# Weight sums pinned in program order, and merge-stage pools that wait tile by tile, in a hybrid encoder block

## The chip, the cores and the metric

The kernel runs on one core of a Trainium2 chip. The time is device microseconds from launch to end; three runs of the kernel before were made, and one more execution was profiled. The engines are TensorE (PE, with its weight loads as PEld), VectorE (DVE), ScalarE (ACT), GpSimd (POOL) and SyncE (SP), which issues all the DMAs here. Each engine takes its instructions in the order in which its queue holds them.

## The reference, cut to what matters

One block of a bidirectional encoder on 1040 tokens (16 meta tokens and 1024 real ones) of width 1024: a normalised input is projected, goes through four heads of chunked retention and through a chunked state-space mixer (SSD) of 32 heads in 4 groups, and the two results are gated, merged, projected and added; then comes a gated feed-forward part with a convolution.

```python
def hybrid_layer(h, pos, norm_mix_w, w_in, ret_gn_w, w_ret_out, ...):
    u = rms_norm(h, norm_mix_w)
    q, k, v, g_ret, z, xbc, dt_f, dt_b, gate_ret, gate_ssd = _split(u @ w_in, IN_SIZES)
    ...
    y_ret = bidirectional_retention(pad_front(q), pad_front(k), pad_front(v), log_gamma)[:, PAD:]
    y_ret = head_group_norm(y_ret).reshape(b, l, RET_V) * ret_gn_w
    y_ret = (jax.nn.silu(g_ret) * y_ret) @ w_ret_out
    ...
    y_ssd = group_rms_norm(y, ssd_norm_w, SSD_GROUPS) @ w_ssd_out
    merged = jax.nn.sigmoid(gate_ret) * y_ret + jax.nn.sigmoid(gate_ssd) * y_ssd
    h = h + merged @ w_out
    f = dw_conv_centred(rms_norm(h, norm_ffn_w) @ w_ffn_up, w_ffn_conv, b_ffn_conv)
    fg, fu = _split(f, (D_FF, D_FF))
    return h + (jax.nn.silu(fg) * fu) @ w_ffn_down
```

## The kernel before

Every float32 product is done as three matmuls on operands split into a high and a low part (`mm3`, lines 143 to 145). A weight is loaded by SP into one of two `wraw` tiles (line 132), split by ACT into `whi` (line 135) and by DVE into `wlo` (line 136), three of each. `fm` makes 8 x 3 matmuls of up to 348 columns into one of three PSUM banks `psd`.

The kernel runs in stages. After the input norm come the four retention heads. The steps of a head's recurrence (`ret_steps`) are interleaved by `merge` with the dense projections of the next head (`ret_dense`; for the last head those of z), by costs that are written into the list. In a head POOL does the product of the rotary sum (`sw`, line 338), the two scalings of q per chunk (`qd`, line 429), and the addition and the power of the chunk's norm (`bs`, lines 448 and 449); DVE makes the normalised chunk `ry` from that (line 451), PE transposes it (`ptr`, line 459), DVE gates it and SP stores it (`yr`, line 467).

The feed-forward product uses sums of blocks of its up-projection weights. They are made in this stage, beside the heads, and kept in DRAM (`ws_d`) until then. `sum_steps` (from line 488) makes them in 44 units: `load` brings two tiles of 128 x 2 x 256 (256 KB each, lines 499 and 500), `add` does four POOL operations in place (lines 506 to 509), `store` writes both tiles back (line 513). The tiles have two buffers each. `spread` puts the steps of 12 units evenly among the dense steps of each of the heads 0 to 2 and the remaining 8 units among those of head 3, with a cost of 0.

The program text is not the order on the engines. A scheduler walks the program with a model of the chip's times and lets each engine issue, at each moment, the earliest traced instruction that is ready in the model; an instruction whose inputs the model takes as landed can go ahead of work that is traced before it. `tc.keep_in_program_order(ins)` ties an instruction behind the one that was traced just before it on its engine, for the order of issue alone.

After the heads comes SSD, group by group, whose last steps for a chunk write `yt` tiles (ACT, line 912) and store them to `ys_d` (line 914). Gate projections (`gate_steps`, lines 291 and 292) run beside it; six steps of them (`last_gates`) are kept for the change to the merge stage. There `kblock` loads the retention result in halves into three `ka` buffers (line 983), ACT casts them to `krh` (line 984) and DVE makes `krl` (line 985), eight tiles each; then `gated` does the product with `w_ro` and scales it by the gate (line 995), and the two SSD products follow, then `w_o` with the residual rows `xr`.

SBUF room is taken in pools that open and close. With the default, the first use of a new pool waits until every earlier pool that held any of its bytes is done with; with `reuse_waits="tile"` each tile waits for the earlier tiles on its own bytes alone. By the sizes in order of allocation, `sg` (the `ka` and `gt` tiles) lies on the bytes of `tok`; `hb` on the end of `tok`, `dec` and the first SSD tiles; `krh` on `bt`, `ct`, `x0`, `x1`, `x2` and `yb`; `krl` on `br`, then the small tiles and `t1` (tile 3 and 4), the two `yt` buffers (tiles 4 and 5), and room of the convolution that is long done. The pools of the feed-forward part (`ob`, `wx`, `fp`) have `reuse_waits="tile"` already.

Of the kernel before, what the change touches and what calls it, by code (L numbers as in the profile page):

```python
# [12 lines left out]
ALU = mybir.AluOpType  # L13
# [82 lines left out]
def hybrid_kernel(ctx, tc, t):  # L96
    nc = tc.nc
# [84 lines left out]
    ws_d = [dr.tile([P, 2, 1024], F32, name=f"ws_{j}", tag=f"ws_{j}") for j in range(NF)]  # L182
# [305 lines left out]
    def sum_steps(us):  # L488


        steps = []

        def part(src, s_):
            return src.rearrange("p (h s c) -> p s h c", h=2, s=2)[:, s_]

        def load(u):
            j, s_ = u // 2, u % 2
            a, b = [rb[0].tile([P, 2, 256], F32, name=f"ws{i}", tag=f"ws{i}", bufs=2) for i in range(2)]
            nc.sync.dma_start(out=a, in_=part(t["w_up"][j], s_))
            nc.sync.dma_start(out=b, in_=part(t["w_up"][NF + j], s_))  # L500
            wsum[u] = a, b

        def add(u):
            a, b = wsum[u]
            a11, a12, a21, a22 = a[:, 0, :], a[:, 1, :], b[:, 0, :], b[:, 1, :]
            nc.gpsimd.tensor_tensor(a22, a21, a22, op=ALU.add)
            nc.gpsimd.tensor_sub(a21, a11, a21)  # L507
            nc.gpsimd.tensor_sub(a11, a22, a11)
            nc.gpsimd.tensor_sub(a12, a12, a11)

        def store(u):
            for i, x in enumerate(wsum.pop(u)):
                nc.sync.dma_start(out=part(ws_d[u // 2][:, i, :], u % 2), in_=x)

        for u in us:
            if u == 0:
                steps += [(0.0, lambda: load(0)), (0.0, lambda: load(1))]
            steps += [(0.0, lambda u=u: add(u)), (0.0, lambda u=u: store(u))]
            if u + 2 < 2 * NF:
                steps.append((0.0, lambda u=u: load(u + 2)))  # L520
        return steps
# [441 lines left out]
    cv_es.close()  # L963
    ssd_es.close()
    tp.close()
    sg = ctx.enter_context(tc.tile_pool(name="sg", bufs=2))
    hp = ctx.enter_context(tc.tile_pool(name="hp", bufs=1))
    hb = hp.tile([P, KT, NB + 2], F32, name="hb")
    nc.gpsimd.memset(hb[:, :, NB:NB + 2], 0.0)
    h2 = [hb[:, d, :] for d in range(KT)]  # L970
    phL = ExitStack()
    lp = phL.enter_context(tc.tile_pool(name="lp", bufs=1))
    HN = NB // 2

    def kblock(pool, name, src):
# [23 lines left out]
    run(last_gates[1:])  # L999
    phA.close()  # L1000
    phR = ExitStack()
    bp = phR.enter_context(tc.tile_pool(name="bp", bufs=1, side="right"))
    for d in range(KT):
        w = wload(t["w_ro"][d])
        for b, (t0, n) in enumerate(BLK_B):
# [11 lines left out]
            sops1 = kblock(lp, "kr", lambda k: ys_d[2 + k // 4][:, k % 4, :])  # L1017
    phR.close()
    phM = ExitStack()
    mp = phM.enter_context(tc.tile_pool(name="mp", bufs=1, side="right"))  # L1020
    mh, ml = [], []
    for d in range(KT):
        w = wload(t["w_so"][2 * d + 1])
# [13 lines left out]


    oa_es = ExitStack()
    oa = oa_es.enter_context(tc.tile_pool(name="oa", bufs=1))  # L1040
    OPS = ("b11", "t2", "t1", "t3", "b21", "t4", "b22")

    def op_tiles(pool, r):
# [2 lines left out]

    ops = [op_tiles(oa, 0), None]
    wo_es = ExitStack()
    wo = wo_es.enter_context(tc.tile_pool(name="wo", bufs=2, side="right"))

    def row_rms(x, n):

# [413 lines left out]
def _build(tc, args):  # L1466
    with ExitStack() as ctx:
        hybrid_kernel(ctx, tc, args)
# [15 lines left out]
```

## Time and profile before

| | |
|---|---|
| median of three runs | 2555.64 us (2548.39 to 2556.68) |
| the profiled execution | 2567.85 us, span 2566.1 us |
| mean granted clock of PE | 0.964 |
| busy share of the span | PE 94%, PEld 88%, DVE 51%, ACT 33%, POOL 30% |
| mean DMA traffic | 126 GB/s |

All rows are times of the one profiled execution, in us from the start of its span. The heads run from about 50 to 535 us, SSD to about 1440, the merge stage to about 1800, the feed-forward part to the end. A wait is listed with the engine and line that waited, what it waited for, the sum in us, how often, and the longest.

### The profile page before, as it was taken

What the parts mean: (1) busy time and instruction counts of PE and PEld (TensorE: products, weight loads), DVE (VectorE), ACT (ScalarE), POOL (GpSimd) and SP (SyncE); (2) the same over time, 40 slices, a digit from 0 to 9 for tenths busy, and PEclk for the clock granted to TensorE, in tenths of its full rate; (3) what the DMA queues carried; (4) which work ended last, traced back from release to release, by engine and by line L of the source; (5) the groups of instructions that cost most, each with busy time, mean ns of one, the idle gap of its engine ahead of it and who ended that gap; (6) DMA issues with size and microseconds to landing.
All of it is one profiled execution on the core that took longest, in us unless ns stands there. A gap on an engine that the chain in (4) does not pass through costs nothing.

```text
span 2566.1 us, 39997 instructions
## 1 busy us (share of the span) xinstructions
PE 2405.6 (94%) x15888; PEld 2248.8 (88%) x15888; DVE 1306.4 (51%) x1917; ACT 850.2 (33%) x1462; POOL 782.4 (30%) x933
## 2 busy tenths in 40 slices
PE   7776899999989989999998899999999999999997
PEld 7766799998779878887988799999899999998887
DVE  6122243364563564365346344343797777774435
ACT  4211221133344253244323422122554444442114
POOL 3566622212561462364145112222111111110002
PEclk9988999999989999998999899999999999999998
DMA  4666621212482375157246655335444444454211
GB/s 160 201 217 200 206 68 46 60 54 78 142 176 63 125 163 103 65 168 155 50 134 170 167 166 150 90 95 167 148 144 128 116 119 116 120 170 175 72 44 66
DMA packets 197227, 324.46 MB, mean 126 GB/s; under 512 B 22128, under 2 KB 125040, under 8 KB 192944
## 3 DMA queue, kind: packets, MB, share of 16 engines
q1 hardware_dynamic: 197040, 321.91, 43.4%
q8 instruction: 125, 2.05, 0.3%
q14 instruction: 62, 0.51, 0.1%
HBM read 241.57 MB, written 80.27 MB: 125 GB/s over the span
## 4 chain that ended last, share of the span: by engine, by line
PE 69%; DMA 11%; POOL 8%; DVE 6%; ACT 3%; issue 3%; SPq 1%; POOLq 0%; DVEq 0%; ACTq 0%
PE psu L1194 17%; PE psd L143 12%; PE psd L145 12%; PE psd L144 11%; DMA ws<-in_w_up 4%; PE psw L144 3%; PE psw L145 3%; PE psw L143 3%; DMA br<-row 2%; PE pss L807 1%; POOL ws L507 1%; PE psb L828 1%; PE psy L442 1%; DMA ws<-ws 1%; POOL t L878 1%
## 5 line engine op out<-in xcount | busy, mean ns | idle before, releaser
L143 PE MATMUL psd<-uh,whi 128*128 128x342 f32 (+3 forms) x1376 | 469.9, 342 | 9.6 <-ACT gs L291 5.0
L144 PE MATMUL psd<-ul,whi 128*128 128x342 f32 (+3 forms) x1376 | 448.7, 326 | 0.0
L145 PE MATMUL psd<-uh,wlo 128*128 128x342 f32 (+3 forms) x1376 | 447.7, 325 | 0.0
L135 ACT CAST whi<-wraw 128x1024 fp32r<-128x1024 f32 (+1 forms) x144 | 149.2, 1038 | 510.3 <-PE psd L144 300.9
L136 DVE TENSOR_TENSOR wlo<-wraw,whi 128x1024 fp32r<-128x1024 f32 (+1 forms) x144 | 190.3, 1323 | 206.3 <-ACT whi L135 206.1
L143 PEld LDWEIGHTS psd<-uh,whi 128*128 128x128 f32 (+1 forms) x1376 | 266.4, 194 | 20.4 <-issue 7.9
L144 PEld LDWEIGHTS psd<-ul,whi 128*128 128x128 f32 (+1 forms) x1376 | 265.6, 193 | 7.7 <-issue 7.4
L145 PEld LDWEIGHTS psd<-uh,wlo 128*128 128x128 f32 (+1 forms) x1376 | 264.8, 192 | 0.1
L143 PE MATMUL psd<-whi,uh 128*128 128x256 f32 x768 | 235.7, 307 | 0.4 <-ACT uh L219 0.4
L145 PE MATMUL psd<-whi,ul 128*128 128x256 f32 x768 | 218.5, 285 | 3.2 <-POOL ul L221 2.7
L144 PE MATMUL psd<-wlo,uh 128*128 128x256 f32 x768 | 219.0, 285 | 0.0
L143 PEld LDWEIGHTS psd<-whi,uh 128*128 128x128 f32 x768 | 148.7, 194 | 11.3 <-issue 8.8
L144 PEld LDWEIGHTS psd<-wlo,uh 128*128 128x128 f32 x768 | 148.9, 194 | 6.1 <-issue 5.5
L145 PEld LDWEIGHTS psd<-whi,ul 128*128 128x128 f32 x768 | 148.1, 193 | 3.9 <-POOL ul L221 3.1
L144 PE MATMUL psw<-ahl,whi 128*128 128x512 f32 (+1 forms) x400 | 149.5, 374 | 1.6 <-DVE ahl L1313 1.6
L143 PE MATMUL psw<-ahl,whi 128*128 128x512 f32 (+1 forms) x400 | 147.5, 371 | 0.0
L145 PE MATMUL psw<-ahl,wlo 128*128 128x512 f32 (+1 forms) x400 | 146.6, 368 | 0.0
L143 PE MATMUL psd<-krh,whi 128*128 128x342 f32 x384 | 124.2, 324 | 3.3 <-ACT krh L984 3.3
L144 PE MATMUL psd<-krl,whi 128*128 128x342 f32 x384 | 124.2, 324 | 0.1
L145 PE MATMUL psd<-krh,wlo 128*128 128x342 f32 x384 | 124.0, 323 | 0.0
L1253 DVE SCALAR_TENSOR_TENSOR hb<-hb,vec 128x1024 f32<-128x1024 f32 x88 | 111.2, 1281 | 0.4 <-ACT hb L1249 0.2
L854 DVE TENSOR_TENSOR br<-br,tok 128x2048 f32<-128x2048 f32 (+1 forms) x36 | 83.5, 2319 | 48.9 <-DMA br<-row 48.9
(306 smaller groups left out, 6151.7 us busy)
## 6 DMA issues: line engine op xcount, KB each, us to landing
br<-row SPq DMA_DIRECT2D x32, 1024.0 KB
ws<-in_w_up SPq DMA_DIRECT2D x88, 256.0 KB
ws<-ws SPq DMA_DIRECT2D x88, 256.0 KB
gt<-gate SPq DMA_DIRECT2D x72, 171.0 KB
wraw<-in_w_xbc SPq DMA_DIRECT2D x24, 512.0 KB
wraw<-ws SPq DMA_DIRECT2D x47, 256.0 KB
hb<-ws SPq DMA_DIRECT2D x45, 256.0 KB
act<-hb SPq DMA_DIRECT2D x22, 512.0 KB
```

What stands on the lines that cost most here:

```text
L135: nc.scalar.copy(hi[:, :n], raw[:, :n])
L136: nc.vector.tensor_sub(lo[:, :n], raw[:, :n], hi[:, :n].bitcast(F32))
L143: nc.tensor.matmul(ps, ah, bh, start=(i == 0), stop=False)
L144: nc.tensor.matmul(ps, ah, bl, start=False, stop=False)
L145: nc.tensor.matmul(ps, al, bh, start=False, stop=(i == n - 1))
L442: nc.tensor.matmul(py[:n, :256], a, b, start=(i == 0), stop=(i == len(mms) - 1))
L507: nc.gpsimd.tensor_sub(a21, a11, a21)
L807: nc.tensor.matmul(ps, bk(c), st[("xw", d, c)][:n], start=True, stop=True)
L828: nc.tensor.matmul(ps[:n, :], tk("ct", c - 1), st[("pb", c)], start=True, stop=True)
L854: nc.vector.tensor_tensor(r, r, tok[:n, c, 0, g * 16:g * 16 + 16].unsqueeze(2).broadcast_to([n, 16, n]), op=ALU.add)
L1194: nc.tensor.matmul(ps[:, :n], a[:, c], b[:, k, :], start=start and k + i == 0, stop=k == 3 and i == 2, skip_group_check=True)
L1253: nc.vector.scalar_tensor_tensor(o[half], f[half][:, 1 + tap:1 + tap + SEQ], V("fconv_w", 3 * fi + tap), o[half], op0=ALU.mult, op1=ALU.add)
```

## The change

Each unit's first POOL addition and both its stores are pinned behind the instruction traced before them on POOL and on SP. The loads and the other three POOL operations are as before. Seven pools that open at or after the change from SSD to the merge stage (`sg`, `hp`, `lp`, `bp`, `mp`, `oa`, `wo`) get `reuse_waits="tile"`. No operation is added or removed.

```diff
         def add(u):
             a, b = wsum[u]
             a11, a12, a21, a22 = a[:, 0, :], a[:, 1, :], b[:, 0, :], b[:, 1, :]
-            nc.gpsimd.tensor_tensor(a22, a21, a22, op=ALU.add)
+            tc.keep_in_program_order(nc.gpsimd.tensor_tensor(a22, a21, a22, op=ALU.add))
             nc.gpsimd.tensor_sub(a21, a11, a21)
             nc.gpsimd.tensor_sub(a11, a22, a11)
             nc.gpsimd.tensor_sub(a12, a12, a11)
 
         def store(u):
             for i, x in enumerate(wsum.pop(u)):
-                nc.sync.dma_start(out=part(ws_d[u // 2][:, i, :], u % 2), in_=x)
+                tc.keep_in_program_order(nc.sync.dma_start(out=part(ws_d[u // 2][:, i, :], u % 2), in_=x))
...
-    sg = ctx.enter_context(tc.tile_pool(name="sg", bufs=2))
-    hp = ctx.enter_context(tc.tile_pool(name="hp", bufs=1))
+    sg = ctx.enter_context(tc.tile_pool(name="sg", bufs=2, reuse_waits="tile"))
+    hp = ctx.enter_context(tc.tile_pool(name="hp", bufs=1, reuse_waits="tile"))
...
-    lp = phL.enter_context(tc.tile_pool(name="lp", bufs=1))
+    lp = phL.enter_context(tc.tile_pool(name="lp", bufs=1, reuse_waits="tile"))
...
-    bp = phR.enter_context(tc.tile_pool(name="bp", bufs=1, side="right"))
+    bp = phR.enter_context(tc.tile_pool(name="bp", bufs=1, side="right", reuse_waits="tile"))
...
-    mp = phM.enter_context(tc.tile_pool(name="mp", bufs=1, side="right"))
+    mp = phM.enter_context(tc.tile_pool(name="mp", bufs=1, side="right", reuse_waits="tile"))
...
-    oa = oa_es.enter_context(tc.tile_pool(name="oa", bufs=1))
+    oa = oa_es.enter_context(tc.tile_pool(name="oa", bufs=1, reuse_waits="tile"))
...
-    wo = wo_es.enter_context(tc.tile_pool(name="wo", bufs=2, side="right"))
+    wo = wo_es.enter_context(tc.tile_pool(name="wo", bufs=2, side="right", reuse_waits="tile"))
```

## Rows read from the trace of the kernel before

**Rows 1.** The page's 40 slices of 64 us: PE busy and granted clock, in tenths.
```profile
PE   7776899999989989999998899999999999999997
PEclk9988999999989999998999899999999999999998
```
**Rows 2.** Windows: length, busy us (instructions) of PE, PEld, DVE, ACT, POOL; clock, DMA share, GB/s.
```profile
75.00:325.00 250.00, 188.50 (x1180) 175.99 (x1179) 64.18 (x147) 49.28 (x106) 159.24 (x230) 0.90 0.67 208
325.00:525.00 200.00, 199.68 (x1351) 189.10 (x1350) 77.67 (x203) 40.87 (x90) 44.93 (x92) 0.99 0.18 53
```
**Rows 3.** Tile ws: ns min/median/max, first and last start; then POOL's idle time before it.
```profile
L506 POOL TENSOR_TENSOR ws<-ws x44: 721/733/1713, 57.8 to 315.4; 128x256 f32<-128x256 f32 x44
...
  DMA ws<-in_w_up: 85.6, 46
```
**Rows 4.** Windows of the three longest stalls of PE in the heads.
```profile
117.50:135.00 17.50, 0.59 (x4) 0.19 (x2) 0.95 (x2) 2.05 (x5) 9.60 (x14) 0.65 0.64 189
182.50:190.00 7.50, 0.00 (x0) 0.00 (x0) 0.55 (x2) 0.00 (x0) 5.19 (x10) 0.84 0.71 236
242.50:260.00 17.50, 0.91 (x3) 0.51 (x4) 3.17 (x8) 0.55 (x2) 10.27 (x18) 0.59 0.65 172
```
**Rows 5.** Waits from 75 to 325 us, of DVE and PE: us in total, times, longest.
```profile
DVE ry L451 <- POOL bs L449: 90.7, 12, 11.6
DVE rk L339 <- POOL sw L338: 45.0, 7, 18.8
...
PE ptr L459 <- DVE ry L451: 36.3, 10, 13.1
```
**Rows 6.** Timeline of POOL: start, us, operation, [idle before it and what ended it].
```profile
123.78 0.72 POOL L506 TENSOR_TENSOR ws<-ws 128x256 f32<-128x256 f32 x1 [3.27 <-DMA ws<-in_w_up]
...
127.55 0.92 POOL L338 TENSOR_TENSOR sw<-sw,sin 128x348 f32<-128x348 f32 x1
```
**Rows 7.** Waits of SP's DMA queue over the whole span.
```profile
SPq L467 <- DVE ryt L465: 58.0, 13, 7.8
```
**Rows 8.** Pieces of the chain that ended last: start, us, what (a store, a load).
```profile
90.27 3.62 DMA ws<-ws
93.91 5.95 DMA ws<-in_w_up
```
**Rows 9.** Timelines of POOL and DVE around one long add.
```profile
173.95 1.63 POOL L507 TENSOR_TENSOR ws<-ws,ws 128x256 f32<-128x256 f32 x1 [1.13 <-DMA ws<-in_w_up]
...
173.77 2.90 DVE L136 TENSOR_TENSOR wlo<-wraw,whi 128x1024 fp32r<-128x1024 f32 x2
```
**Rows 10.** Windows at the change to the merge stage and after it.
```profile
1447.50:1455.00 7.50, 2.54 (x12) 2.26 (x11) 2.54 (x4) 2.95 (x5) 0.11 (x1) 0.70 0.21 35
1455.00:1465.00 10.00, 10.00 (x57) 9.73 (x57) 4.66 (x7) 4.92 (x9) 0.00 (x0) 0.88 0.86 250
1465.00:1472.50 7.50, 4.09 (x14) 3.01 (x13) 3.69 (x5) 3.78 (x8) 0.00 (x0) 0.67 0.83 239
1472.50:1480.00 7.50, 7.50 (x34) 7.50 (x33) 2.22 (x4) 2.82 (x5) 0.00 (x0) 0.65 0.69 217
1480.00:1800.00 320.00, 320.00 (x2159) 320.00 (x2158) 125.34 (x181) 70.16 (x98) 72.62 (x79) 1.00 0.45 134
```
**Rows 11.** Chain that ended last, at the change to the merge stage.
```profile
1438.75 12.53 DMA ys<-yt
1451.37 0.63 ACT krh L984
...
1452.81 3.40 DMA ka<-yr
...
1457.60 3.63 DMA ka<-yr
```
**Rows 12.** Timeline of SP's DMA queue: the first loads of the retention result.
```profile
1431.10 1.54 SPq L983 DMA_DIRECT2D ka<-yr  x3
```
**Rows 13.** Waits of PE from 1420 to 1480 us.
```profile
PE psd L143 <- ACT gs L291: 5.0, 1, 5.0
```

## The prediction

> **What bounds the kernel now.** I read the 40 slices of the page first: the reader is to see that TensorE (PE) is busy at nine tenths nearly everywhere, and that the exceptions are the first five slices (to 320 us), a few eights later, two of them side by side (1411 to 1540 us), and the last slice; the granted clock is below full in most of these [rows 1]. So the end is set by PE, and an edit is worth what PE idles, or does at its lower clock, in the stage it touches.
>
> The windows view puts numbers on the retention stage. From 75 to 325 us PE is busy 188.5 of 250 us at a granted clock of 0.90, and DMA stands at 0.67; from 325 to 525 us, with the same kind of work for heads 2 and 3, PE is busy 199.7 of 200 [rows 2]. What differs is where the 44 weight sums lie: the first add starts at 57.8 us and the last unit at 315.4 [rows 3], although the program text spreads them over all four heads. So before the change the sums ran ahead, 257.6 / 43 = 6.0 us a unit.
>
> Why does that stop PE? Three long stalls carry 41 of the 61.5 us [rows 4]. The waits of that stretch name VectorE (DVE) waiting for GpSimd (POOL): the normalised chunk waits 90.7 us for the power on POOL, the rotary sum 45.0 us for POOL's product, and PE's transpose waits for the chunk [rows 5]. POOL's own order shows the reason: the rotary product of 127.55 us stands behind adds that had to wait for their loads [rows 6], and POOL waits for those loads 46 times, 85.6 us [rows 3]. POOL takes its queue in order, so whatever stands behind such an add is late.
>
> **Part 1, the adds and stores pinned.** The first add of each unit goes behind the POOL instruction traced before it, which hangs on PE's progress through its head, and so does each store on SP. The other three adds depend on the first; the two loads are not pinned, but with two buffers the load of unit u+2 needs the stores of unit u landed. So loads, adds and stores of all units are spread. No work is removed: 176 adds, 88 loads, 88 stores remain. The bound of the gain is what PE loses now. Idle: 61.5 us. Clock: 250 x (1 - 0.90) = 25 us of deficit, of which the three stalls hold 17.5 x 0.35 + 7.5 x 0.16 + 17.5 x 0.41 = 14.5 us, where PE was idle anyway; about 10 us were matmuls at the lower level. Sum 71 us.
>
> What is late next? After the change the stage would last from 57.8 to 525 - 71 = 454, or 396 / 44 = 9.0 us a unit, against the 6.0 us at which the chain of units can run. The loop of a buffer pair is: four adds of 0.73 us, 2.9 [rows 3]; on SP the store stands behind a yr store, which now makes the queue wait 13 times, 58.0 / 13 = 4.5 us each, 7.8 at most [rows 7]; a store landing 3.6 and a load 6.0 [rows 8]. Without the yr wait that is 12.5 us, near the present 2 x 6.0; with it 17.0 us against two units, 18.0: it fits, narrowly; at 7.8 it is 20.3, and the add stands waiting 2.3 us. Queued behind that add on POOL are the power of the chunk, the rotary product and the two scalings of q; DVE waits for the first two, PE for DVE. How much wait does PE not see? Before, DVE waited 90.7 / 12 = 7.6 us each time and PE 36.3 / 10 = 3.6 [rows 5], so some 4 us are covered; and from 325 us on PE loses nothing although the same chain runs there [rows 2]. One unit of 2.9 us is covered. Unit plus 2.3 is 5.2, so 1.2 us too long. If every unit did that, 44 x 1.2 = 53 us would come back and 18 us of gain remain; if none did, 71. I take the 13 units whose queue now waits for a yr store: 13 x 1.2 = 16 us, a gain of 55 us.
>
> The DMAs move too: the traffic that made 0.67 goes into a stretch at 0.18 [rows 2], which only shortens landings. Weight loads that stand behind a pinned store wait one unit's adds, 2.9 us; their cover is the three split weights ahead of PE, each 72 matmuls (36 to 72 for the token-major ones), 5 to 11 us at 320 / 2159 = 0.148 us [rows 10], so nothing; without that cover it would be 2.9 us for each load that meets one. The last unit ends before the last yr stores in program order, and those are waited for already when the next stage opens; nothing there.
>
> A rule of the Trainium skill speaks against the spreading. The row first: an add that meets a two-input subtraction on DVE took 1.63 us instead of 0.73 [rows 9, 3]. The page "SBUF — State Buffer", section "SBUF: two separate sides", says that DVE and GpSimd share one port pair as an exclusive lock, which a DVE operation with two SBUF inputs takes against a GpSimd operation that reads SBUF. The trace agrees for those adds. By the rule alone, adds placed beside DVE's work would all be long; that is a rival below.
>
> **Part 2, pools that wait tile by tile.** Two PE gaps at the change of stage: 1447.5 to 1455 us (busy 2.5 of 7.5) and 1465 to 1472.5 (4.1 of 7.5), and matmuls at the lower clock behind each [rows 10]. The chain shows a ys store of 12.53 us, and then the first cast of krh [rows 11]. Its input had been issued at 1431.10 [rows 12]; it waited for the whole SSD pool, whose yt tiles that store reads. ScalarE stood with it, and behind it on ScalarE the gate that frees a PSUM bank: PE waited 5.0 us for that [rows 13]. By room, krh0 to krh3 and krl0 to krl3 lie on tiles done by about 1430; only krl4 and krl5 lie on yt. So casts can start at 1431.1 + 3.4 = 1434.5 [rows 11, 12]. Then the three buffers of ka turn over once in 1457.60 - 1452.81 = 4.8 us [rows 11]: sixteen halves are 5.3 turns, 26 us, done at 1460.5, or 1465 if the ys stores slow the loads by 4.5 us (my estimate, a turn). The gates without a stall end at 1465 - 5.0 (idle) - 1.2 (10 us at a clock of 0.88 [rows 10]) = 1459. By 1480 the retention product has done 14 + 34 matmuls, less some 4 of the last gate, at 0.148 us [rows 10], 6.5 us of work, so it began in effect at 1473.5; after, between 1461 and 1467 with 2 us for a clock fallen once. Gain 6 to 12, I take 9. Ends: 14 if the clock stays up and krh is ready at 1459; minus 5 if the casts, now early in ScalarE's queue, wait for ka with the gates behind them, as one did for 5.0 us. For the pools of the products that follow (right-hand ones, the sums' operands, the x rows) I take nothing: PE is busy 320 of 320 us there [rows 10], and these waits end beneath it. Were that cover gone, the same 5 us would be the price.
>
> **Sum.** 55 + 9 = 64 us. The profiled execution took 2567.85 us (span 2566.1 and 1.75 around it), so 2504 in its terms; it lies 12.2 us above the median of the runs, 2555.64, so I predict 2491.6, said as 2491.
>
> **Rivals.** (a) The sums still bunch, because only the first add is pinned and the loads are free: then part 2 alone, 9 us, 2547. Against: the add's predecessor hangs on PE. (b) Long adds: all four at 1.63 us, a unit 6.5 us and the loop 20.6, 10.3 us a unit, 44 x 10.3 = 453 us instead of 396; 57 of 71 come back, total gain 14 + 9, 2533. Against: DVE's weight subtractions are few beside 176 adds, and the median is 0.73 [rows 3]. (c) Slower: the SP queue becomes the clock. A store waits for its add, the load behind it for the store, the next pinned add for the load, all of them behind yr stores. It decides from the point where a unit takes more than the present (525 - 57.8) / 44 = 10.6 us. With two yr waits of 7.8 us in one loop (28.1 us a pair) for half of the pairs and 17.0 for the rest it is 11.3 us a unit, 497 us instead of 467: 30 more, less 9 of part 2, 2577. For it: SP is one queue. Against: 36 yr stores for 44 units, so two in one loop are rare.
>
> **How the numbers follow.** Chances: my forecast with anything between 13 and 85 us gained 0.78, (a) 0.06, (b) 0.06, (c) 0.07, more than the bound 0.03. The forecast's own bounds are 71 + 14 = 85 us, 2470.6, and 18 - 5 = 13 us, 2542.6; (b) lies within, (a) a little outside. As the runs shown scatter 7 us downwards, I say 2465 to 2541. A measurement of this kernel tells about 0.3%, 7.7 us, from no change; (a) lies at that edge, half of it counts as same, as does a thin edge of the forecast. Faster 0.87, same 0.06, slower 0.07.
>
> **What would show it.** Part 1: the adds' first and last start should reach from about 60 to 440 us or more, PE from 75 to 325 should be busy over 240 of 250 at a clock near 1, and the wait of the chunk for the power should fall from 7.6 us each to under 4. If instead POOL waits for the sums' loads more than 85.6 us, the loop does not fit and (c) is near. Part 2: the first krh cast should start before the last ys store lands, some 17 us earlier against its neighbours than now, and PE's 5.0 us wait for the gate should be gone. What makes the prediction wrong is a residue of waits in heads 0 and 1, the least known term.

## The result, and the profile after

The changed kernel took 2495.15 us (median; 2493.57 to 2498.12), the kernel before on the same chip 2555.84: a ratio of 0.977, interval 0.9749 to 0.9791. The prediction was 2491, with a range of 2465 to 2541. The profiled execution of the changed kernel took 2496.15 us, with a span of 2494.4, and so lies 1 us above its median; that of before lay 12 us above its own. The traces are therefore 71.7 us apart where the medians are 60.7 apart.

The page's slices of PE and its granted clock after the change; [rows 1] has them before:

```profile
PE   7999999989899989989998899999899999999997
PEclk9999999999999989999999999999999999999998
```

The second to fifth slice now stand at nine tenths or more in both lines. Windows of the same two stretches as [rows 2], in the same columns:

```profile
75.00:325.00 250.00, 243.07 (x1604) 232.10 (x1603) 87.64 (x200) 62.50 (x139) 131.07 (x198) 0.99 0.52 160
325.00:525.00 200.00, 188.94 (x1283) 179.48 (x1282) 88.95 (x189) 48.46 (x90) 83.07 (x160) 0.98 0.46 133
```

PE is busy 243.07 of 250 us at a clock of 0.99. The DMA share is even over both stretches, and POOL's work has moved with the sums. (The second stretch now reaches 40 us into SSD; of PE's 11 us of idle time in it, 6.5 lie there.) The tile ws, and POOL's idle time before it, as in [rows 3]; then the waits of DVE and PE from 75 to 325 us, as in [rows 5]:

```profile
L506 POOL TENSOR_TENSOR ws<-ws x44: 721/734/745, 103.2 to 460.7; 128x256 f32<-128x256 f32 x44
...
  DMA ws<-in_w_up: 53.9, 16
```

```profile
DVE ry L451 <- POOL bs L449: 44.7, 18, 11.7
...
PE ptr L459 <- DVE ry L451: 6.3, 1, 6.3
```

The sums now run from 103 to 461 us, 8.3 us a unit instead of 6.0. The chunk waits for the power 2.5 us each time instead of 7.6, and PE's transposes wait 6.3 us in sum instead of 36.3.

To see where the 71.7 us of the spans arose, I take three instructions of both traces: the start of line 627 (DVE's first step of SSD), the start of the last copy of `yt` (line 912), and the last scaling by the gate in the retention product (line 995).

| start, us | line 627 | last line 912 | last line 995 | span |
|---|---|---|---|---|
| before | 544.7 | 1438.0 | 1742.7 | 2566.1 |
| after | 484.3 | 1370.6 | 1670.5 | 2494.4 |
| gained by then | 60.4 | 67.4 | 72.2 | 71.7 |

The heads gave 60.4 us, SSD 7.0, the change to the merge stage 4.8, the rest nothing. The 7.0 us of SSD aren't a gain: the change has no part in that stage, and the order of the instructions on each engine there is the same in both traces. From the first to the second of these instructions the traces of before and after take 893.3 and 886.3 us, and nine kernels below that leave this stage as it is (e1 to e5, e9, e11, e12, e14) take 887.4 to 898.2.

The chain that ended last, at the change to the merge stage, as in [rows 11]:

```profile
1363.47 6.24 DMA ys<-yt
1369.79 1.15 ACT yt L912 x4
1370.94 0.52 ACT krh L984
1371.48 0.71 DVE krl L985
1372.20 13.06 DMA ka<-yr
...
1386.66 3.25 DMA ka<-yr
```

The first cast of krh no longer waits for the last ys store. But the next batch of ka loads takes 13.06 us where one took 3.40 before.

### The profile page after: what moved, and what is told of

Its sections match the earlier page's. It is cut to its first block, busy times and chain, and to the rows that moved or that the text cites. A ratio compares the mean times of both kernels' runs of the same rounds, so it can differ in the third digit from the quotient of the medians.

```text
span 2494.4 us, 39978 instructions
## 1 busy us (share of the span) xinstructions
PE 2384.2 (96%) x15888; PEld 2234.1 (90%) x15888; DVE 1309.5 (52%) x1917; ACT 849.6 (34%) x1462; POOL 785.8 (32%) x933
## 4 chain that ended last, share of the span: by engine, by line
PE 68%; DMA 9%; POOL 8%; DVE 6%; ACT 3%; issue 3%; SPq 1%; POOLq 0%; DVEq 0%; ACTq 0%
PE psu L1194 17%; PE psd L143 12%; PE psd L145 12%; PE psd L144 12%; PE psw L144 3%; PE psw L145 3%; PE psw L143 3%; DMA br<-row 2%; DMA ws<-ws 2%; DMA ws<-in_w_up 2%; POOL t L878 2%; PE pss L807 1%; PE psb L828 1%; DMA ka<-yr 1%; DVE br L854 1%
## 5 line engine op out<-in xcount | busy, mean ns | idle before, releaser
L143 PE MATMUL psd<-uh,whi 128*128 128x342 f32 (+3 forms) x1376 | 464.7, 338 | 4.8 <-ACT gs L291 3.8
L1338 DVE TENSOR_TENSOR hb<-psw,hb 128x512 f32<-128x512 f32 x80 | 55.2, 691 | 103.7 <-PE psw L145 103.7
```

The lines of the kernel that those rows point to most:

```text
L143: nc.tensor.matmul(ps, ah, bh, start=(i == 0), stop=False)
L1338: nc.vector.tensor_tensor(hs, ps, hs, op=ALU.add)
```

## Experiments: the two parts alone

e1 has the pins alone, without `reuse_waits="tile"` in the seven pools:

```diff
-    sg = ctx.enter_context(tc.tile_pool(name="sg", bufs=2, reuse_waits="tile"))
+    sg = ctx.enter_context(tc.tile_pool(name="sg", bufs=2))
...
```

> The adds and stores are pinned, the seven pools are as before. Theory: the retention stage carries the gain. The change from retention to SSD came 60.4 us earlier in the profile of after, of which I count 56 as gain and the rest as scatter between executions, so 2500 us (2495 to 2505), and PE busy over 240 of 250 us from 75 to 325. Rival (the pools carry more than the 5 us that the merge stage shows): 2515 or more.

e2 has the pools alone, without the two `tc.keep_in_program_order`:

> The seven pools wait tile by tile, nothing is pinned; the order on every engine is that of before. Theory: 5 us less than before, 2551 us, the first krh cast at or before the last ys store lands, and the retention stage unchanged (PE busy about 188 of 250 from 75 to 325). Rival 1 (my prediction's term): 9 us, 2547. Rival 2 (the ys stores hold the loads of ka as long as they held the casts): 0, 2556.

Measured, beside the kernel before at 2565.59 us: e1 2512.02 us, ratio 0.9793 (0.977 to 0.9816); e2 2562.22 us, 0.9984 (0.9972 to 0.9997). The parts are worth 53.6 and 3.4 us, 57.0 together; the whole change is worth 60.7 us on its first chip and 56.3 on another (2510.04 against 2566.38, ratio 0.9773, 0.9756 to 0.979). Within the intervals they add, and part 1 carries nearly all. (e1 had been expected to give 56 us, e2 to give 5.)

> The changed kernel as it is, beside the three others of this group. It should stand at 0.975 to 0.979 of the kernel before, with PE busy 242 to 244 of 250 us between 75 and 325 us, as in its first trace, and with the second batch of ka loads taking 12 to 14 us behind the last ys stores. If those numbers move by more than 5 us from execution to execution, the readings of single traces in this study are worth less than I make of them.

That second execution of the changed kernel tells the scatter of single traces. PE is busy 240.64 of 250 us between 75 and 325 us, and line 627 starts at 490.4 instead of 484.3. Over the five traces with the same program of the heads (after, e1, e11 and, below, e7 and e13) it starts at 484.3 to 494.2, 489.4 on average. Single traces of one program thus lie up to 10 us apart in this stage, and I read nothing from smaller differences between two of them.

## Experiments: which pin does it

e3 is the changed kernel with the stores free again; only the first add of each unit is pinned:

```diff
-                tc.keep_in_program_order(nc.sync.dma_start(out=part(ws_d[u // 2][:, i, :], u % 2), in_=x))
+                nc.sync.dma_start(out=part(ws_d[u // 2][:, i, :], u % 2), in_=x)
```

> After without the pin on the stores: they and the loads may go as soon as their unit is added. POOL's order is that of after, SP's is not. Theory (POOL's order is what costs): as after within 5 us, 2490 to 2500, and POOL waits less for the loads of the sums than the 53.9 us of after, because no store stands behind a yr store. Rival (the order of the stores on SP, ahead of the weight loads, is what costs): near 2545, as before but for the merge stage.

e4 is the changed kernel with the adds free again; only the stores are pinned:

> After without the pin on the adds: the stores hold the loads by the two buffers, but adds may go up to two units ahead of their place on POOL. Theory (POOL's order is what costs): part of the gain, 2500 to 2530, with POOL waiting more for loads than the 53.9 us of after and the chunk waiting more for the power than 77.5 us. Rival (the order of the stores on SP is what costs): as after, 2495.

Measured: e3 2493.59 us, ratio 0.972 (0.9701 to 0.9739); e4 2555.06 us, 0.9958 (0.9943 to 0.9974). As e3 had come out below the changed kernel's ratio, both ran once more on one chip:

> The changed kernel with the stores free again and only the first add of each unit pinned, a second time, now on the same chip as the changed kernel. Theory: the pin on the stores costs time, because on SP a pinned store stands between the loads of the next unit and the queue: the adds wait 54 us for their loads with it, 39 us without. Then this version is 8 to 12 us below the changed kernel (the first dt_xx at 474 against 484 us, PE busy 249 of 250). Rival: the 0.972 of its first runs against 0.977 is the difference of two chips: then it is within 3 us of the changed kernel.

Measured: 2494.20 us, ratio 0.9713 (0.9695 to 0.9731), against 2510.04 of the changed kernel: the pin on the stores costs 15.8 us, more than the 8 to 12 expected. This version beats both kernels. The order on POOL, ScalarE, DVE and PE is the same in both, instruction for instruction; only SP's differs. The windows of e12, in the same columns:

```profile
75.00:325.00 250.00, 248.39 (x1656) 235.94 (x1655) 89.88 (x208) 62.84 (x141) 134.96 (x204) 1.00 0.55 164
```

Most of the difference arises at one place, the changed kernel's longest stall of the heads, from 250 us on; all five traces of its program have it. Behind it the changed kernel is 8.3 us later than e12, of 9.4 by the end of the heads (in e11 9.1 of 15.5). The same window of the changed kernel and of e12:

```profile
240.00:270.00 30.00, 23.70 (x131) 22.91 (x130) 13.02 (x31) 4.57 (x9) 15.70 (x24) 0.89 0.53 167
...
240.00:270.00 30.00, 29.04 (x180) 27.93 (x179) 13.46 (x37) 5.64 (x11) 19.07 (x31) 1.00 0.66 187
```

There the changed kernel does 131 matmuls where e12 does 180, by idle time and by the lower clock behind it. First SP's DMA queue, then POOL, in the changed kernel:

```profile
229.58 0.56 SPq L500 DMA_DIRECT2D ws<-in_w_up  x1
242.55 0.88 SPq L513 DMA_DIRECT2D ws<-ws  x2
244.69 0.55 SPq L499 DMA_DIRECT2D ws<-in_w_up  x1
```

```profile
235.96 0.74 POOL L509 TENSOR_TENSOR ws<-ws 128x256 f32<-128x256 f32 x1
...
240.92 1.60 POOL L509 TENSOR_TENSOR ws<-ws 128x256 f32<-128x256 f32 x1
...
250.42 0.72 POOL L506 TENSOR_TENSOR ws<-ws 128x256 f32<-128x256 f32 x1 [7.48 <-DMA ws<-in_w_up]
```

SP stood 12.3 us at a pinned store, until the adds of 240.92 us had ended; the load behind it left at 244.69, and POOL stood 7.48 us at the next add, with the powers behind it; PE waited 6.30 us for the chunk. In e12 the same add starts at 244.6 us instead of 250.4, and the next unit's at 259.4 instead of 267.7. The sums of the waits don't show this: POOL waits 53.9 us for the sums' loads in the changed kernel and 51.6 in e12, and from 75 to 525 us SP even stands longer at the stores in e12 (67.4 us for line 507 and 39.0 for line 509, against 66.3 for line 509). But there no wait for an add lasts over 4.9 us, where the pinned stores have one of 12.3. Why the store wasn't released when an earlier unit's adds ended at 236.7 the trace doesn't tell; that stays open.

e4 shows the opposite case. The tile ws, and POOL's idle time before it:

```profile
L506 POOL TENSOR_TENSOR ws<-ws x44: 721/732/1712, 56.7 to 507.1; 128x256 f32<-128x256 f32 x44
...
  DMA ws<-in_w_up: 145.7, 42
```

The sums are spread even further, 10.5 us a unit, and yet PE is busy only 219.5 of 250 us from 75 to 325. The adds stand somewhat earlier in POOL's queue than in the changed kernel (36 ahead of the first power of a chunk, against 16; before the change 73), while their loads now come at the pace of the pinned stores; POOL stands at them 145.7 us, against 53.9 with the adds pinned too. Neither expectation had this: they were 2500 to 2530 us, and 2495. So spreading alone doesn't pay: what pays is an add that stands so late in POOL's queue that POOL seldom waits long at it.

## Experiments: what cost PE its time before

The prediction blamed adds that wait for loads at the head of POOL's queue. Three kernels made from the kernel before take away the wait, the work, and both.

e9 lets the adds work on a small tile of their own:

```diff
-            a, b = wsum[u]
-            a11, a12, a21, a22 = a[:, 0, :], a[:, 1, :], b[:, 0, :], b[:, 1, :]
+            if u == 0: kept.append(rb[0].tile([P, 256], F32, name="wk", tag="wk", bufs=1)); nc.vector.memset(kept[0], 0.0)
+            a11 = a12 = a21 = a22 = kept[0]
```

> The kernel before, with no pin and no change to the pools; the four additions of each unit work on a small tile of their own instead of on the loaded tiles, so the sums that are stored are the weights as loaded, and the feed-forward part computes with those. All 176 additions stay, in size and number, all 88 loads and 88 stores too; only the wait of an addition for its loads is gone. Theory, the head of POOL's queue: PE lost 61.5 us because POOL stood 85.6 us at additions whose loads were under way; without that wait PE is busy over 240 of 250 us between 75 and 325 us, the heads end 50 to 65 us earlier than before, and the time is about 0.975 to 0.98 of the kernel before, although the additions now come in one bunch. Rival, POOL's own work: 44 x 2.9 us of additions in a bunch delay the power and the rotary product as well, and PE stays below 215 of 250. Rival, DMA traffic: the loads and stores of the sums at a share of 0.67 delay the weights; they bunch as much as before, so PE stays at about 190.

e14 makes them 8 columns wide:

```diff
-            a11, a12, a21, a22 = a[:, 0, :], a[:, 1, :], b[:, 0, :], b[:, 1, :]
+            a11, a12, a21, a22 = a[:, 0, :8], a[:, 1, :8], b[:, 0, :8], b[:, 1, :8]
```

> The kernel before; the four additions of each unit take 8 columns of their tiles instead of 256, so most of the stored sums are the weights as loaded, and the feed-forward part computes with those. The order on the engines is that of the kernel before: each addition stands where it stood and waits for its loads as it did, but takes some 0.1 us instead of 0.73, so POOL is free of 100 to 115 of its 159 busy us between 75 and 325 us. It tells apart which half of POOL's full queue (159 us of work and 86 us of waits in 250) costs PE its time. Theory, the waits: PE stays at 190 to 215 of 250 and the time at 0.985 or more of the kernel before. Rival, the work: POOL catches up behind each wait, PE is busy over 235 of 250 us, and the time is 0.975 to 0.98.

e5 leaves the four lines 506 to 509 out:

> The kernel before with the four additions of each unit left out; the loads and the stores of the weight sums stay and now run ahead freely, so the stored sums are the weights as loaded, and the feed-forward part computes with those. Theory, POOL's queue: with nothing of the sums on POOL, PE is busy over 245 of 250 us between 75 and 325 us at a clock near 1, whatever the DMA share, and the time is 0.972 to 0.976 of the kernel before, which is what pinning can reach at most in this stage. Rival, DMA traffic: loads and stores at a share of 0.67 or more delay the weights, and PE stays below 230.

Measured, with the windows from 75 to 325 us of e9, e14 and e5, one fence each:

```profile
75.00:325.00 250.00, 178.92 (x1144) 169.63 (x1144) 66.55 (x140) 46.27 (x101) 131.01 (x210) 0.86 0.64 202
```

```profile
75.00:325.00 250.00, 210.57 (x1326) 198.78 (x1325) 70.06 (x170) 50.30 (x109) 73.07 (x235) 0.92 0.67 207
```

```profile
75.00:325.00 250.00, 234.18 (x1517) 222.87 (x1516) 83.52 (x196) 59.97 (x131) 47.74 (x86) 0.97 0.67 213
```

| | time, us | ratio | line 627 starts |
|---|---|---|---|
| before | | 1 | 544.7 |
| e9, no wait for loads | 2572.58 | 1.0028 (1.0014 to 1.0042) | 549.9 |
| e14, adds of 8 columns | 2536.31 | 0.9882 (0.9865 to 0.9899) | 519.5 |
| e5, no adds | 2512.14 | 0.9796 (0.9782 to 0.9811) | 489.7 |
| e12, only adds pinned | 2494.20 | 0.9713 (0.9695 to 0.9731) | 474.9 |

e9 went against my theory. With nothing to wait for, the adds all went ahead, from 52 to 187 us, and filled POOL by their work alone; all 176 stood ahead of the first power of a chunk, where 73 did before. Windows of e9:

```profile
150.00:175.00 25.00, 0.00 (x0) 0.00 (x0) 1.34 (x2) 1.51 (x4) 22.37 (x36) 0.50 0.00 0
...
225.00:250.00 25.00, 25.00 (x152) 24.06 (x152) 11.79 (x29) 5.13 (x9) 8.17 (x15) 1.00 0.87 273
```

From 150 to 175 us PE did nothing while POOL was busy 22.4 of 25 us; between 50 and 325 us DVE waited 99.3 us for the rotary product (75.2 and 24.1, for `rk` and `rq`). So waiting for loads isn't needed: a bunch of adds ahead of the heads' small POOL steps can cost PE as much by work as by waiting. The second line bears on the third rival: with the adds over and DMA at 0.87, PE is full. Of PE's 71 idle us in e9, 66.6 lie before 200 us, beside the adds, and 4.5 after, though the sums' loads and stores go on to 311 us.

e14 kept the waits (POOL stood 150.5 us at lines 506 and 507 for loads) and cut each add from 0.73 to 0.20 us. The order isn't quite that of before: the scheduler put the adds up to 12 places further ahead. The heads ended 25 us earlier; PE's 210.57 us lie at the upper edge of what the theory of the waits allowed. e5 took the rest away and gained 30 us more, but PE stopped at 234 of 250, between what the two accounts said. Its longest stall tells why; timelines of SP's queue, POOL and PE in e5:

```profile
197.25 4.84 SPq L513 DMA_DIRECT2D ws<-ws  x4
202.13 0.47 SPq L416 DMA_DIRECT2D qdc<-in_qdec  x1
```

```profile
207.31 1.04 POOL L429 TENSOR_TENSOR qd<-rq,qdc 128x16 f32<-128x16 f32 x3 [19.80 <-DMA qdc<-in_qdec]
```

```profile
209.94 0.69 PE L459 MATMUL ptr<-cst,ry 128*128 128x128 f32 x2 [10.41 <-DVE ry L451]
```

SP stood at four stores of sums whose loads were still under way (58.6 us in 63 such waits from 50 to 325 us), and behind them stood a small load of the heads' decay factors. POOL waited 19.80 us for it, the chunk's power stood behind that, and PE waited 10.41 us. The load landed some 5 us after its issue, as in the other heads and runs (3.6 to 5.5 us), so its landing wasn't the long part. Of PE's 15.8 idle us in the window, 13.1 lie at this stall. So the bunch of loads and stores costs time by SP's queue, without any add. With the adds back in and everything spread (e12) the heads end another 15 us earlier. So of the 70 us between before and e12 the work of the adds holds some 25, their waits with the rest of their work 30, and the bunch of loads and stores 15, in this order of taking them away. In another order they come out otherwise: e9 took the waits away first and gained nothing. Each figure is the difference of two single traces, which scatter by up to 10 us; the ratios of the runs give 30, 22 and, less what the pools give in e12, 17.

## Experiments: where the merge stage's gain went

e7 is the changed kernel with the last two ys stores issued by ScalarE:

```diff
-            nc.sync.dma_start(out=ys_d[g][:, :, s:s + m], in_=yt[:, :, :m])
+            (nc.scalar if g == G - 1 and c >= NC - 2 else nc.sync).dma_start(out=ys_d[g][:, :, s:s + m], in_=yt[:, :, :m])
```

> The changed kernel; only the last two ys stores of the last group are issued by ScalarE instead of SyncE. Theory, order in the queue: the second batch of ka loads took 13.06 us because it stands behind the ys stores in SP's DMA queue. On another queue the loads take 4 to 6 us, the first scaling by the gate of the merge stage (line 995) comes 3 to 7 us earlier, and the time is 3 to 7 us below the changed kernel. Rival, shared engines: the 16 DMA engines are busy with the small packets of the ys stores whatever the queue; the loads still take 10 us or more and the time is within 2 us.

e10 has this edit on e3:

> Both of the two preceding edits at once: stores free, and the last two ys stores issued by ScalarE. The two lie 900 us apart and should add: 11 to 19 us below the changed kernel if both theories hold (about 0.970 of the kernel before), 8 to 12 us below if only the pin on the stores costs, 3 to 7 us below if only the queue of the ys stores does.

Measured: e7 2510.31 us, ratio 0.9775 (0.9759 to 0.9792), against 2510.04 of the changed kernel beside it; e10 2495.86 us, 0.9726 (0.9708 to 0.9745), against 2494.20 of e12. No change in either, and the batch of ka loads still takes 12.78 us in e7's chain. The rival held: the engines are shared. DMA traffic of e7 from 1388 to 1402 us (busy tenths of the engines and GB/s in 40 slices; queues with packets, MB and their share of the 16 engines):

```profile
DMA  9787889999999999999999989989899969989979
GB/s 197 207 268 197 240 303 383 404 449 422 372 329 358 272 227 177 122 81 48 59 49 82 69 69 105 135 88 91 32 60 63 56 63 140 137 110 166 208 153 198
...
q1 hardware_dynamic: 1137, 1.98, 67.7%
q10 hardware_dynamic: 1050, 0.52, 42.4%
```

q10 is ScalarE's queue and holds the two ys stores alone: 0.52 MB in 1050 packets of about 500 bytes take 42.4% of 14 us, the time of 5.9 us on all 16 engines; q1 moved nearly four times the bytes in 9.5 us. (The two shares add up to 110%, so packets of the two queues overlap in time, and 5.9 us isn't time that the stores held the engines alone.) While the stores pass, the engines are as busy as before at 32 to 135 GB/s. The Trainium skill says the same in "DMA: Bandwidth & Descriptors", section "Issuing engines are not separate DMA queues": DMAs of several issuing engines end on the same 16 engines, and a second issuer saves only issue time. Here 13.06 against 12.78 us agree with it.

e13 moves these stores out of that moment:

```diff
-            nc.sync.dma_start(out=ys_d[g][:, :, s:s + m], in_=yt[:, :, :m])
+            for s_ in [s] * (g < G - 1 or c < NC - 2) + [s + CH * (NC - 4)] * (g == G - 1 and c in (2, 3)): nc.sync.dma_start(out=ys_d[g][:, :, s_:s_ + m], in_=yt[:, :, :m])
```

> The changed kernel; in the last group the last two chunks of ys aren't stored, and two earlier chunks (2 and 3) are stored to their place as well, some 60 us earlier, so the last 256 columns of that group carry the values of other tokens. The number of stores is the same; 0.5 MB of small packets leaves the moment at which the merge stage opens. Theory, engines filled by small packets: the second batch of ka loads, 13 us in the changed kernel, takes 4 to 6 us, the first scaling by the gate comes 5 to 8 us earlier behind the last yt than in the changed kernel, and the time is 4 to 8 us below it (0.974 to 0.9755 of the kernel before). Rival: the weights of w_ro, the gate rows and the ka loads themselves fill the engines there; the loads stay above 10 us and the time is within 2 us of the changed kernel. A second rival: the loads get faster, but the casts and the gates on ScalarE, or the gates' own work on PE, end last by then, and the time moves less than 3 us.

Measured: 2504.80 us, ratio 0.9761 (0.9738 to 0.9784). The chain of e13:

```profile
1385.32 0.52 ACT krh L984
...
1387.18 5.57 DMA ka<-yr
...
1394.16 4.54 DMA ka<-yr
...
1400.10 3.36 DMA ka<-yr
```

The batch that took 13.06 us takes 5.57; with e7, which leaves out the queue as the reason, this says that the small packets did fill the engines. The first scaling by the gate comes 27.7 us behind the last copy of `yt`, against 37.5 in the changed kernel, and PE no longer waits for the gate; but its waits for the casts grew from 2.2 to 4.9 us, so the second rival held in part. From the last copy of `yt` to the last scaling of the retention product it is 295.7 us in e13, 299.9 to 303.3, on average 301.2, in the eight other traces with tile-wise pools (after, e2, e3, e4, e7, e10, e11, e12), and 303.4 to 304.7, on average 304.2, in the five without (before, e1, e5, e9, e14). So part 2 gained 3.0 us there, and e13 gave 5.5 more. That this is the transfers' doing alone isn't shown, because in e13 the scheduler also put the steps of SP, ScalarE and PE in another order there. The ratio's interval overlaps that of the changed kernel; the time alone doesn't settle it.

## Why the prediction was right, and where it was not

The forecast was a gain of 64 us, 55 by part 1 and 9 by part 2. In medians the whole change gained 60.7 us; e1 alone gained 53.6 and e2 alone 3.4.

**The bound of part 1 held.** It was 71 us of idle time and low clock, read from one window of before. With only the adds pinned, line 627 starts at 474.2, 474.9 and 472.1 us in e3, e12 and e10, 71.0 us before that of the kernel before: PE recovers all of it.

**The residue had the right size and the wrong carrier.** I predicted 16 us of remaining waits, and a gain of 55; the five traces of the pinned program end the heads 55.3 us earlier than before, 15.7 us short of the bound. I had let the store wait behind a yr store, 13 times by 1.2 us. The runs show that the pin on the stores is the whole residue, since the heads without it end at the bound; but it lies mostly in one stall, not in 13 steps, and there the store itself waits for adds, with the next load behind it. (For the term I had read one of SP's rows for the yr stores, 58.0 us in 13 waits, and left out the one beside it, `SPq L467 <- DVE rs L423: 60.4, 9, 29.1`; after the change no yr store holds SP for more than 6.1 us.) That is the mechanism of my rival (c) in small, and the agreement of the sizes is partly luck. The single steps were off as well: the first add starts at 103 and not about 60 us, because it is pinned behind a rotary product that waited 24.57 us for ScalarE, and a unit takes 8.3 us where I had 9.0.

**The cause was only half told.** I read the 85.6 us of waiting [rows 3] as the reason and passed over POOL's 159.24 busy us from 75 to 325 us [rows 2]. In that window the waits are these, in the form of [rows 3]:

```profile
  DMA ws<-in_w_up: 76.1, 43
```

The two make 235 of 250 us: POOL was nearly full. e9 shows that the work alone can cost as much as before, and e14 that some 25 to 30 us went with less work although the waits stayed. And that the DMAs move too, "which only shortens landings", was priced at nothing; e5 puts it at about 15 us, by what the heads themselves load and store behind the bunched sums on SP's queue.

**Part 2 was sized too high.** Predicted 9 us with 6 to 12; e2 measured 3.4 in medians, and the traces show 3.0. Two steps failed. First, I let the casts start at 1434.5 us, but on ScalarE they stand behind the last copies of `yt`. Timelines of ScalarE, before and then after:

```profile
1437.23 1.14 ACT L912 ACTIVATE yt<-pty,vec 128x128 f32<-128x128 f32 x4
1451.37 1.66 ACT L984 CAST krh<-ka 128x513 fp32r<-128x513 f32 x3 [13.00 <-DMA ys<-yt]
```

```profile
1369.79 1.15 ACT L912 ACTIVATE yt<-pty,vec 128x128 f32<-128x128 f32 x4 [1.24 <-DMA ys<-yt]
1370.81 1.68 ACT L984 CAST krh<-ka 128x513 fp32r<-128x513 f32 x3
```

The casts came 13 us earlier, all that this queue allowed, and not 17. Second, a turn of the ka buffers was put at 4.8 us, with one turn more for the ys stores. The first turn took 14.5 us (1372.20 to 1386.66), since the stores are on the engines at just that time: the wait for a transfer became a wait for another transfer behind it. The last ys store's own 12.53 us, with no ka load issued beside it [rows 11], could have warned me. PE's wait for the gate is 3.8 us in the changed kernel (6.5 in e11), not gone. The whole gain came within 4 us of the forecast because part 1 was sized nearly right and is most of it.

**The rivals.** (a), the sums still bunch, is out by the adds' 103 to 461 us. (b), long adds, is out too: 3 of 176 adds take over 1.2 us in the changed kernel, against 10 before. Two of the three, at 239.24 and 240.92 us, 1.60 each instead of 0.73, lie beside a weight subtraction of DVE (238.61 us, two in 3.32), so the trace agrees again with the lock that the Trainium skill states in "SBUF — State Buffer", section "SBUF: two separate sides"; it matters little, since there are few such meetings. (c), SP as the clock, doesn't hold in the changed kernel, with 8.3 us a unit against its limit of 10.6; e4 reaches 10.5 and keeps almost nothing of the gain. Two small misreadings of [rows 1] have no bearing on the sum: of the ten weak slices that I named, five and not most show a clock below 0.9, and the two side by side lie at 1347 to 1475 us, not 1411 to 1540.

## What to carry to other kernels

Add an engine's busy time to its waits at the head of its queue, in the stage's own window: where the sum comes near the window, as 235 of 250 us here, suspect the side work that a scheduler let run ahead, whether it waits or works. Pin the one operation that holds up the others in the queue, here the add, and leave its transfers free; a pinned store kept the loads behind it waiting too, for 15.8 us here. Before a removed wait is counted as a gain, look at what stands ahead in the same queue and which transfers share the engines at that moment.

## What was not expected of the hardware

Two stores of 256 KB in packets of about 500 bytes, whose time adds up to 5.9 us on all 16 DMA engines, were in the way of a load of 256.5 KB: it landed after 13.06 us where 3.40 had been seen [rows 11], and after 5.57 us with these stores moved away (e13). A queue of another issuing engine changed nothing (12.78 us). A high DMA share by itself didn't slow PE: in e9 PE was busy 25.0 of 25 us at a share of 0.87. What hurt in e5 was one small load behind the sums' stores on SP's queue.
